# Both banks of a row tile in one loop over k, the second matmul of each pair asked to use the weights already in the array

## Chip, cores, metric

One core of a Trainium2 chip. The metric is the device time of one execution in microseconds (us); medians over several executions are quoted.

## The reference

```python
m, k, n = 4096, 4096, 4096
a, b, bias = randn(m, k), randn(k, n), randn(n)      # float32
out = np.tanh(np.matmul(a, b) + bias)
```

## The kernel before

The operands are cast to fp16 by the DMAs that load them. `a` is transposed on VectorE (DVE) and is the stationary operand: 128 x 128 weights per k tile, 32 k tiles (`KT`). `b` is the moving operand: a chunk of 1024 columns lies in SBUF, as `J` = 2 pieces of `NB` = 512 columns, for one `ps` tile in PSUM each (a bank, below). After a special start for the first eight row tiles, 120 row tiles follow (`todo`). Each takes one bank after the other: 32 matmuls of 512 columns into the first bank, 32 into the second. The k-th matmuls of both banks use the same weights, and each loads them for itself.

```python
    def mm(ps, at, bt, t, j, start, stop):
        nc.tensor.matmul(
            ps, at[:, t, :], bt[t // TB][:, t % TB, ts(j, NB)], start=start, stop=stop
        )

    def finish(ps, addend, mi, c0, w=NB, o_sb=None, pieces=1):
        ...                                  # DVE: add the bias out of PSUM; ACT: tanh; SP: store
    # ... the start: warm-up matmuls, first column chunk ...
    for i, (c, mi) in enumerate(todo):
        # ... loads of b and a for later row tiles ...
        if i + 2 < len(todo):
            new_at(i + 2)                    # DVE: transpose of the row tile after the next
        at = at_q.pop(0)
        for j in range(J):
            halves = 2 if i == len(todo) - 1 and j == J - 1 else 1
            w = NB // halves
            for h in range(halves):
                ps = psum.tile([P, w], fp32, name="ps")
                c0 = j * NB + h * w
                for t in range(KT):
                    nc.tensor.matmul(
                        ps,
                        at[:, t, :],
                        b_cur[t // TB][:, t % TB, ds(c0, w)],
                        start=t == 0,
                        stop=t == KT - 1,
                    )
                finish(ps, bias_bc[:, ds(c0, w)], mi, c * NCW + c0, w, pieces=halves)
```

## Time and profile before

| | before |
|---|---|
| time | 1792.26 us, median of 3 runs (1791.81 to 1792.65) |
| matmuls, weight loads in the trace | 8248, 8248 |
| start of one matmul to start of the next, 300 to 1700 us | 215 or 216 ns, mean 215.83 ns |
| 512 columns alone, at 0.4167 ns a column (2.4 GHz; worked out of four widths below) | 213.33 ns |

The page of the profile of before. The line of engines gives busy us, share of the span and number of instructions (PE is TensorE's matmuls, PEld its weight loads). q8 is the queue that brings instructions (packets, MB). The long line is the chain of waits that ended last, by share of the span. Then groups: line, engine, operation, output<-input, shapes, count, then busy us and mean ns of one, then idle time before.

```profile
span 1789.8 us, 19352 instructions
...
PE 1779.1 (99%) x8248; PEld 807.4 (45%) x8248; DVE 745.0 (42%) x420; ACT 162.7 (9%) x260; POOL 358.0 (20%) x668
...
q8 instruction: 64, 1.05, 0.2%
...
PE ps L321 92%; PE ps L121 2%; DMA b<-in_b_dram 2%; DMA an<-in_a_dram 1%; POOL b L66 0%; DMA bias_bc<-in_bias_dram 0%; POOL an L75 0%; DVE atx L83 0%; ACT o_sb L135 0%; DVE o_sb L132 0%; ACTq L354 0%; DVEq L132 0%; POOLq L343 0%
...
L321 PE MATMUL ps<-b,at 128*128 128x512 f16 x7712 | 1657.8, 378 | 0.0
L321 PEld LDWEIGHTS <-at 128*128 128x128 f16 x7712 | 754.6, 98 | 903.3
L132 DVE TENSOR_TENSOR o_sb<-ps,bias_bc 128x512 f32<-128x512 f32 (+1 forms) x243 | 166.4, 686 | 977.8 <-PE ps L321 764.1
```

The chain is 92% the matmuls of L321, the row tiles, and TensorE never idles there (0.0 us before the 7712 matmuls). A matmul's record lasts 378 ns in the mean, while matmuls start 215.83 ns apart: the records overlap, so their length says nothing about the rate. The rate is in the starts. This is the timeline of before between 500 and 503 us (start, duration, engine, group, count):

```profile
499.77 3.40 PE L321 MATMUL ps<-b,at 128*128 128x512 f16 x15
499.99 2.90 PEld L321 LDWEIGHTS <-at 128*128 128x128 f16 x14
```

Fifteen matmuls span 3.40 us, the last one's record of 379 ns included: (3.40 - 0.379) / 14 = 0.2158 us from start to start. The fourteen weight loads keep the same step, one for each matmul, 98 ns each.

VectorE's part of the timeline of before shows the order of its work, one addition per bank, some 6.9 us apart:

```profile
493.99 0.69 DVE L132 TENSOR_TENSOR o_sb<-ps,bias_bc 128x512 f32<-128x512 f32 x1 [1.86 <-issue]
500.89 0.69 DVE L132 TENSOR_TENSOR o_sb<-ps,bias_bc 128x512 f32<-128x512 f32 x1 [6.21 <-PE ps L321]
501.50 4.43 DVE L83 STREAM_TRANSPOSE at<-an 128x4096 f16<-128x4096 f16 x1
```

### The profile page before, as it was taken

The page shows a single profiled execution, that of the slowest core. Times are in us where ns is not written, and L with a number is a line of the kernel's source. Part 1 is how long each engine was busy: PE and PEld are TensorE (multiplying, and loading weights), DVE is VectorE, ACT ScalarE, POOL GpSimd, SP SyncE. Part 2 cuts the span into 40 slices and gives each one's busy share as a digit, 9 for nine tenths or more (in the row PEclk, how much of TensorE's full clock was granted, in tenths as well). Part 3 has the DMA queues.
Part 4 walks back from the last instruction along what each step waited for, and adds up shares of the span by engine and source line. Part 5 has one row for each costly group of instructions (what it writes and reads, how often), then busy time and mean ns, then how long its engine had stood idle before and what let it go on. Part 6 is the DMA issues. An engine that isn't in the chain of part 4 may idle for free.

```text
span 1789.8 us, 19352 instructions
## 1 busy us (share of the span) xinstructions
PE 1779.1 (99%) x8248; PEld 807.4 (45%) x8248; DVE 745.0 (42%) x420; ACT 162.7 (9%) x260; POOL 358.0 (20%) x668
## 2 busy tenths in 40 slices
PE   8999999999999999999999999999999999999999
PEld 3444444444444444444444444444444444444444
DVE  5463344334433444334433443344334433444341
ACT  0110000000000000000000000000000000000001
POOL 6422222211222211111132222111111111111100
PEclk9999999999999999999999999999999999999999
DMA  9999887665777865655588777555665555655621
GB/s 182 214 189 189 155 159 147 125 132 114 159 147 144 170 140 108 121 119 124 106 168 156 158 142 142 121 112 107 127 120 112 112 113 109 125 112 111 120 70 41
DMA packets 138630, 238.26 MB, mean 133 GB/s; under 512 B 14769, under 2 KB 27569, under 8 KB 138545
## 3 DMA queue, kind: packets, MB, share of 16 engines
q0 software_dynamic: 101248, 169.91, 56.6%
q1 hardware_dynamic: 37296, 67.13, 10.3%
q8 instruction: 64, 1.05, 0.2%
q14 instruction: 22, 0.17, 0.0%
HBM read 337.64 MB, written 67.11 MB: 226 GB/s over the span
## 4 chain that ended last, share of the span: by engine, by line
PE 95%; DMA 4%; POOL 1%; issue 1%; DVE 0%; ACT 0%; ACTq 0%; DVEq 0%; POOLq 0%
PE ps L321 92%; PE ps L121 2%; DMA b<-in_b_dram 2%; DMA an<-in_a_dram 1%; POOL b L66 0%; DMA bias_bc<-in_bias_dram 0%; POOL an L75 0%; DVE atx L83 0%; ACT o_sb L135 0%; DVE o_sb L132 0%; ACTq L354 0%; DVEq L132 0%; POOLq L343 0%
## 5 line engine op out<-in xcount | busy, mean ns | idle before, releaser
L321 PE MATMUL ps<-b,at 128*128 128x512 f16 x7712 | 1657.8, 378 | 0.0
L321 PEld LDWEIGHTS <-at 128*128 128x128 f16 x7712 | 754.6, 98 | 903.3
L132 DVE TENSOR_TENSOR o_sb<-ps,bias_bc 128x512 f32<-128x512 f32 (+1 forms) x243 | 166.4, 686 | 977.8 <-PE ps L321 764.1
L83 DVE STREAM_TRANSPOSE at<-an 128x4096 f16<-128x4096 f16 (+1 forms) x136 | 551.0, 4056 | 26.7 <-DMA an<-in_a_dram 26.7
L75 POOL DMA_DIRECT2D an<-in_a_dram x524 | 282.8, 547 | 1296.6 <-DVE at L83 1224.4
L135 ACT ACTIVATE o_sb<-o_sb 128x512 f32<-128x512 f32 (+1 forms) x243 | 151.5, 624 | 1505.7 <-DVE o_sb L132 1505.7
L66 POOL DMA_DIRECT2D b<-in_b_dram x136 | 73.2, 542 | 55.2 <-PE ps L321 28.6
L121 PE MATMUL ps<-b,at 128*128 128x512 f16 x256 | 58.6, 391 | 3.9 <-DMA b<-in_b_dram 2.9
L121 PE MATMUL ps<-b,atx 128*128 128x512 f16 x256 | 55.7, 379 | 1.3 <-DVE atx L83 1.3
L121 PEld LDWEIGHTS <-at 128*128 128x128 f16 x256 | 25.3, 100 | 37.1 <-issue 5.7
L121 PEld LDWEIGHTS <-atx 128*128 128x128 f16 x256 | 24.8, 98 | 32.2 <-DVE atx L83 2.7
L132 DVE TENSOR_TENSOR spill<-ps,spill 128x512 f32<-128x512 f32 x16 | 10.7, 684 | 25.7 <-PE ps L121 25.4
L135 ACT ACTIVATE spill<-spill 128x512 f32<-128x512 f32 x16 | 10.0, 630 | 117.2 <-DVE spill L132 117.2
L83 DVE STREAM_TRANSPOSE atx<-an 128x1024 f16<-128x1024 f16 (+1 forms) x8 | 18.3, 2295 | 0.0
L155 DVE TENSOR_TENSOR spill<-ps,bias_bc 128x512 f32<-128x512 f32 x16 | 10.1, 670 | 10.0 <-PE ps L121 10.0
L196 PE MATMUL ps<-zeros 128*128 128x512 f16 x24 | 7.3, 476 | 1.2 <-DVE zeros L193 1.2
L196 PEld LDWEIGHTS <-zeros 128*128 128x128 f16 x24 | 2.8, 118 | 5.2 <-issue 2.5
L90 POOL DMA_DIRECT2D bias_bc<-in_bias_dram x4 | 2.3, 563 | 0.1
L135 ACT ACT_TABLE_LOAD x1 | 1.3, 1283 | 0.7 <-PEq L343 0.7
L193 DVE MEMSET zeros<- 128x256 uint32 x1 | 0.3, 272 | 0.9 <-PEq L343 0.9
L343 POOL MEMSET const-float32-0.0<- 128x1 f32 x1 | 0.1, 98 | 0.2 <-issue 0.2
L343 POOL MEMSET const-bfloat16-1.0<- 128x1 bf16 x1 | 0.1, 101 | 0.0
(2 smaller groups left out, 0.2 us busy)
## 6 DMA issues: line engine op xcount, KB each, us to landing
an<-in_a_dram POOLq DMA_DIRECT2D x492, 256.0 KB, 5.4
out_dram<-o_sb SPq DMA_DIRECT2D x239, 256.0 KB, 4.3
b<-in_b_dram POOLq DMA_DIRECT2D x120, 256.0 KB, 8.9
out_dram<-spill SPq DMA_DIRECT2D x16, 256.0 KB, 6.4
an<-in_a_dram POOLq DMA_DIRECT2D x16, 192.0 KB, 7.8
an<-in_a_dram POOLq DMA_DIRECT2D x16, 128.0 KB, 5.7
b<-in_b_dram POOLq DMA_DIRECT2D x16, 128.0 KB, 5.0
bias_bc<-in_bias_dram POOLq DMA_DIRECT2D x4, 512.0 KB, 8.2
```

The costliest lines, as they stand in the source:

```text
L66: nc.gpsimd.dma_start(out=bt[t0 // TB][ds(q * QP, QP), ds(t0 % TB, nt), :], in_=src.rearrange("(t p) n -> p t n", p=QP),)
L75: nc.gpsimd.dma_start(out=an[ds(q * QP, QP), :, :], in_=src.rearrange("(mb p) k -> p mb k", p=QP),)
L83: nc.vector.transpose(at[:, ds(t0, nt), :].rearrange("P t (mb p) -> P mb t p", p=QP), an[:, ds(mb0, Q), :].rearrange("P mb (t k) -> P mb t ...
L90: nc.gpsimd.dma_start(out=bias_bc, in_=bass.AP(tensor=src.tensor, offset=src.offset, ap=[[0, P], *src.ap]),)
L121: nc.tensor.matmul(ps, at[:, t, :], bt[t // TB][:, t % TB, ts(j, NB)], start=start, stop=stop)
L132: nc.vector.tensor_tensor(out=o_sb[:, piece], in0=ps[:, piece], in1=addend[:, piece], op=mybir.AluOpType.add)
L135: nc.scalar.activation(o_sb[:, piece], o_sb[:, piece], mybir.ActivationFunctionType.Tanh)
L155: nc.vector.tensor_tensor(out=aside(m, j), in0=ps, in1=bias_bc[:, ts(j, NB)], op=mybir.AluOpType.add)
L193: nc.vector.memset(zeros, 0.0)
L196: nc.tensor.matmul(warm, zeros[:, :P], zeros, start=i == 0, stop=i == WARM - 1)
L321: nc.tensor.matmul(ps, at[:, t, :], b_cur[t // TB][:, t % TB, ds(c0, w)], start=t == 0, stop=t == KT - 1,)
L343: nc = _bacc.Bacc("TRN2", target_bir_lowering=False, num_devices=1)
```

## The change

Take both banks of a row tile through k together, so that the two matmuls with the same weights follow each other, and spare the second its weight load. The second is put in by hand as an instruction with `ldweights=False`. The last row tile stays as it was.

```diff
+    def mm_held(ps, at, bt, t, j, start, stop):
+
+        rhs = bt[t // TB][:, t % TB, ts(j, NB)]
+        nc.tensor.add_instruction(
+            mybir.InstMatmult(
+                name=nc.get_next_instruction_name(),
+                start_tensor_calc=start,
+                stop_tensor_calc=stop,
+                tile_size=(P, P),
+                tile_position=(0, 0),
+                ldweights=False,
+                ins=[
+                    nc.tensor.lower_ap(rhs, opt=False),
+                    nc.tensor.lower_ap(at[:, t, :], opt=False, for_matmul_weights=True),
+                ],
+                outs=[nc.tensor.lower_ap(ps)],
+            )
+        )
...
+        if i < len(todo) - 1:
+
+            pair = [psum.tile([P, NB], fp32, name="ps") for j in range(J)]
+            for t in range(KT):
+                mm(pair[0], at, b_cur, t, 0, t == 0, t == KT - 1)
+                mm_held(pair[1], at, b_cur, t, 1, t == 0, t == KT - 1)
+            for j in range(J):
+                finish(pair[j], bias_bc[:, ts(j, NB)], mi, c * NCW + j * NB)
+            continue
```

## The prediction

> What bounds the kernel now. The page of the profile gives TensorE 99% busy, and the chain of waits is 92% steady-state matmuls of the row tiles. Busy time says little for pipelined matmuls, so I read the spacing of their starts in the trace: between 300 and 1700 us they are 215 or 216 ns apart, mean 215.83 ns, with no longer gap even where one bank gives way to the next. The first column, where eight banks alternate, shows the same. The windows view shows a granted clock of 1.00, so 512 columns at 2.4 GHz[...] take 213.33 ns: the array streams 98.8% of the time, and 2.5 ns per matmul is left. The 256-column matmuls of the last piece are 109.2 ns apart, again 2.5 ns over their columns: a fixed cost per matmul. From 127.8 to 1782.1 us there is nothing but matmuls back to back; the rest is the start and some 8 us of tail, which the change leaves alone.

> What the change removes. 119 of 120 row tiles are paired: 119 x 32 = 3808 weight loads go. One takes 98 ns by the line's view, 373 us of 807 us in sum. But each starts 1.6 ns after a matmul starts and ends over 115 ns before the next: all hidden, so removing it gains nothing by itself. The only thing to win is the part of the 2.5 ns that belongs to changing weights, at most 3808 x 2.5 = 9.5 us (0.53%). [...] at the halved clock the first matmuls, which load weights too, are 426 or 427 ns apart, 512 columns at 1.2 GHz with nothing added; an array-side switch of six cycles would add 5 ns. So I expect a matmul without a load to cost the same 215.8 ns. No matmul of before goes without a load, which leaves it open.

> What the change moves. Both banks of a row tile end 0.2 us apart, not 6.9. VectorE then adds twice in a row (0.69 us each), ScalarE does two tanh (0.62), two stores go out together. VectorE is 42% busy and its order is unchanged, so the next transpose starts some 0.5 us later, with two row tiles (27.6 us) of slack. PSUM is four row tiles deep; no wait. The weights have at least 215 ns for a load of 98 ns. Tiles of b are released at most half a row tile earlier or later, double buffered. The last row tile is as before.

> On the critical path: only the spacing of the matmuls. Predicted 1791.5 us, range 1782 to 1794. Chances: faster by over 2% 0.01, within 2% 0.97, slower 0.02.

> What would show each step: some 4440 weight loads, busy near 434 us; matmul count as before; spacing of starts after a loaded and after a held matmul both 215.8 ns (if 213.3 for the held ones, then some 1783 us); no idle TensorE at row-tile ends; VectorE additions in pairs.

> What would make it wrong: a held matmul that cannot follow its neighbour as closely (each 10 ns would cost 38 us), a weight load that is not pulled ahead past a held matmul and is exposed, or extra semaphore waits from instructions put in by hand.

(1791.5 us is the time of before, measured at 1792.26 us, with nothing taken off for the loads, and the 1782 us of the range are those 1791.5 us less the 9.5 us. The 2.4 GHz were not read from a trace then, but the trace of before gives them: 215.83 ns at 512 columns less 109.17 ns at 256 (mean of the last 60 steps) are 106.67 ns for 256 columns, 0.4167 ns a column.)

## The result

After: 1791.10 us median of 4 runs (1790.47 to 1791.91). Before, on the same occasion: 1792.03 us (1791.03 to 1792.65, 4 runs). Ratio 0.9996, 95% interval 0.9978 to 1.0013: the same. A ratio here is the mean time of one kernel's fast runs over that of the other's fast runs of the same rounds, so it is not quite the ratio of the medians.

The page of the profile of after, the same parts as above (L121 is the ordinary matmul of a pair and some of the start, L128 the one put in by hand):

```profile
span 1788.7 us, 19352 instructions
...
PE 1777.7 (99%) x8248; PEld 807.2 (45%) x8248; DVE 733.8 (41%) x420; ACT 159.0 (9%) x260; POOL 358.0 (20%) x668
...
q8 instruction: 64, 1.05, 0.2%
...
PE ps L121 52%; PE ps L128 46%; PE ps L349 1%; DMA an<-in_a_dram 1%; DVE atx L83 0%; DVE at L83 0%; DVE spill L174 0%; POOL an L75 0%; ACT o_sb L154 0%; DVE o_sb L151 0%; ACTq L382 0%; DVEq L83 0%; DVEq L151 0%; DVE spill L151 0%; POOLq L371 0%
...
L121 PE MATMUL ps<-b,at 128*128 128x512 f16 x4064 | 1500.6, 379 | 4.2 <-DMA b<-in_b_dram 2.9
L128 PE MATMUL ps<-b,at 128*128 128x512 f16 x3808 | 1443.2, 379 | 0.0
L121 PEld LDWEIGHTS <-at 128*128 128x128 f16 x4064 | 397.6, 98 | 485.7 <-issue 4.7
L128 PEld LDWEIGHTS <-at 128*128 128x128 f16 x3808 | 372.6, 98 | 449.3
...
L151 DVE TENSOR_TENSOR o_sb<-ps,bias_bc 128x512 f32<-128x512 f32 (+1 forms) x243 | 155.0, 680 | 989.0 <-issue 969.5
```

This is the first thing to read, before any time: there are still 8248 weight loads, and 3808 of them carry the line of the matmul that was to have none. The instruction count (19352) and the instruction bytes (1.05 MB) have not moved either. The loop order did change. TensorE's weight loads in the timeline of after take both lines in turn:

```profile
499.93 0.10 PEld L128 LDWEIGHTS <-at 128*128 128x128 f16 x1
500.15 0.10 PEld L121 LDWEIGHTS <-at 128*128 128x128 f16 x1
500.36 0.10 PEld L128 LDWEIGHTS <-at 128*128 128x128 f16 x1
500.58 0.10 PEld L121 LDWEIGHTS <-at 128*128 128x128 f16 x1
```

And VectorE adds twice in a row at the end of each row tile (timeline of after), then transposes:

```profile
485.73 1.29 DVE L151 TENSOR_TENSOR o_sb<-ps,bias_bc 128x512 f32<-128x512 f32 x2 [8.17 <-issue]
486.93 4.43 DVE L83 STREAM_TRANSPOSE at<-an 128x4096 f16<-128x4096 f16 x1
499.54 1.29 DVE L151 TENSOR_TENSOR o_sb<-ps,bias_bc 128x512 f32<-128x512 f32 x2 [8.17 <-issue]
```

The pair takes 1.29 us where two single ones took 0.69 each; that is VectorE's 11 us less busy time (745.0 to 733.8), off the critical path. TensorE has 0.0 us of idle time before L128, and start to start is 215 or 216 ns, mean 215.83 ns, as before.

So the measured "same" answers another question than the one asked: it shows that the loop order costs nothing, and says nothing yet about a matmul without a load.

### The profile page after: what moved, and what is told of

Its sections match the earlier page's. It is cut to its first block, busy times and chain, and to the rows that moved or that the text cites. A ratio compares the mean times of both kernels' runs of the same rounds, so it can differ in the third digit from the quotient of the medians.

```text
span 1788.7 us, 19352 instructions
## 1 busy us (share of the span) xinstructions
PE 1777.7 (99%) x8248; PEld 807.2 (45%) x8248; DVE 733.8 (41%) x420; ACT 159.0 (9%) x260; POOL 358.0 (20%) x668
## 3 DMA queue, kind: packets, MB, share of 16 engines
q8 instruction: 64, 1.05, 0.2%
## 4 chain that ended last, share of the span: by engine, by line
PE 98%; DMA 1%; DVE 1%; issue 0%; POOL 0%; ACT 0%; ACTq 0%; DVEq 0%; POOLq 0%
PE ps L121 52%; PE ps L128 46%; PE ps L349 1%; DMA an<-in_a_dram 1%; DVE atx L83 0%; DVE at L83 0%; DVE spill L174 0%; POOL an L75 0%; ACT o_sb L154 0%; DVE o_sb L151 0%; ACTq L382 0%; DVEq L83 0%; DVEq L151 0%; DVE spill L151 0%; POOLq L371 0%
## 5 line engine op out<-in xcount | busy, mean ns | idle before, releaser
L121 PE MATMUL ps<-b,at 128*128 128x512 f16 x4064 | 1500.6, 379 | 4.2 <-DMA b<-in_b_dram 2.9
L128 PE MATMUL ps<-b,at 128*128 128x512 f16 x3808 | 1443.2, 379 | 0.0
L121 PEld LDWEIGHTS <-at 128*128 128x128 f16 x4064 | 397.6, 98 | 485.7 <-issue 4.7
L128 PEld LDWEIGHTS <-at 128*128 128x128 f16 x3808 | 372.6, 98 | 449.3
L151 DVE TENSOR_TENSOR o_sb<-ps,bias_bc 128x512 f32<-128x512 f32 (+1 forms) x243 | 155.0, 680 | 989.0 <-issue 969.5
L154 ACT ACTIVATE o_sb<-o_sb 128x512 f32<-128x512 f32 (+1 forms) x243 | 147.7, 625 | 1509.5 <-DVE o_sb L151 1509.5
L121 PE MATMUL ps<-b,atx 128*128 128x512 f16 x256 | 55.7, 379 | 1.3 <-DVE atx L83 1.3
L121 PEld LDWEIGHTS <-atx 128*128 128x128 f16 x256 | 24.8, 98 | 32.2 <-DVE atx L83 2.7
L349 PE MATMUL ps<-b,at 128*128 128x256 f16 (+1 forms) x96 | 14.1, 308 | 0.0
```

Source lines behind the costliest of these rows:

```text
L121: nc.tensor.matmul(ps, at[:, t, :], bt[t // TB][:, t % TB, ts(j, NB)], start=start, stop=stop)
L128: nc.tensor.add_instruction(mybir.InstMatmult(name=nc.get_next_instruction_name(), start_tensor_calc=start, stop_tensor_calc=stop, tile_si ...
L151: nc.vector.tensor_tensor(out=o_sb[:, piece], in0=ps[:, piece], in1=addend[:, piece], op=mybir.AluOpType.add)
L154: nc.scalar.activation(o_sb[:, piece], o_sb[:, piece], mybir.ActivationFunctionType.Tanh)
L349: nc.tensor.matmul(ps, at[:, t, :], b_cur[t // TB][:, t % TB, ds(c0, w)], start=t == 0, stop=t == KT - 1,)
```

## Experiments

Theory 1: the flag is not honoured when the program is built, so the changed kernel is only a change of loop order. Theory 2: even with the loads really gone nothing is won, because the 2.5 ns over the 512 columns belong to each matmul and not to changing weights. The rivals: the 2.5 ns are the price of changing weights (up to 9.5 us to win); or a load cannot be placed two matmuls ahead and the change would lose time.

All start-to-start figures below are differences of successive matmul starts in the trace between 300 and 1700 us:

```
kernel            columns   loads     mean ns   the commonest steps (count)
before              512      8248      215.83   216 (5402), 215 (1083)
after               512      8248      215.83   216 (5402), 215 (1084)
e0_plain_pairs      512      8248      215.83   216 (5402), 215 (1083)
e1_held             512      4440      215.83   216 (5402), 215 (1083)
e2_one_load         512       751      215.83   216 (5402), 215 (1084)
e3_two_loads        512     15864 *    215.83   216 (5403), 215 (1083)
e4_three_loads      512     23480 *    215.83   216 (5402), 215 (1083)
e5_narrow_loads     128     31096       55.83   56 (20892), 55 (4182)
e6_narrow_held      128      4440       55.83   56 (20893), 55 (4181)
e7_64_loads          64     61560       35.16   29 (31479), 30 (6261), 53 (925)
e8_64_held           64      4440       29.17   29 (40001), 30 (7998)
* in the built program; the trace records 8248
```

### e0: the loop order alone

```diff
-                mm_held(pair[1], at, b_cur, t, 1, t == 0, t == KT - 1)
+                mm(pair[1], at, b_cur, t, 1, t == 0, t == KT - 1)
```

> The changed loop order, but the second matmul of a pair is an ordinary one. Theory (the flag that asks for no load is not honoured when the program is built, so every matmul of the changed kernel still has a load): the built program is the same instruction for instruction as the changed kernel, 8248 weight loads, so 1791 us, within 1 us of the changed kernel. Rival (the flag does something on the chip that the count of loads does not show): a difference from 1791.1 us, or another spacing than 215.8 ns.

A listing of the two built programs was compared first: apart from line numbers, TensorE's instructions are the same in the same order, 8248 loads and 8248 matmuls, and so are those of the other engines. Measured: 1791.47 us (5 runs), ratio to before 1.0 (0.9987 to 1.0012). Theory 1 holds. The changed kernel with `ldweights=True`, and with the flag left away, builds to the same program once more: each time 8248 loads and the flag False on all 8248 matmuls. In these builds the flag changed nothing, whether given as False, as True or not at all.

### e1: the loads really taken out

The changed kernel, with the load before each `mm_held` deleted from the scheduled program (none of these loads held a wait or a signal, which the edit asserts):

```diff
+HELD = set()                       # names of the matmuls that mm_held puts in
+def edit_loads(nc):                # between the schedule and the launch
+    ...                            # for each block: out = [], load = None
+            for i in b.instructions:
+                if isinstance(i, mybir.InstLdweights):
+                    load = len(out)
+                elif isinstance(i, mybir.InstMatmult):
+                    if i.name in HELD:
+                        del out[load]
+                    load = None
+                out.append(i)
+            b.instructions = out
```

> The changed kernel with the 3808 loads really taken out of the scheduled program: 4440 loads, some 434 us of load time. If the 2.5 ns over the 512 columns is a fixed cost of every matmul (theory): spacing stays 215.8 ns, 1791 us, same as before within 0.1%. If it is the price of changing weights (rival 1): 213.3 ns before or after a held matmul, 1791 - 9.5 = 1782 us, 0.9947 of before. If the engine cannot place a load two matmuls ahead (rival 2): spacing over 216 ns at every second matmul, slower than 1795 us. The result must stay correct.

Measured: correct; 1792.36 us (1791.16 to 1794.66, 5 runs), ratio 1.0005 (0.9993 to 1.0018). Its page, the line of engines, and the instruction queue:

```profile
PE 1777.3 (99%) x8248; PEld 434.6 (24%) x4440; DVE 733.8 (41%) x420; ACT 159.0 (9%) x260; POOL 357.9 (20%) x668
...
q8 instruction: 49, 0.80, 0.2%
```

The loads are gone this time: 3808 fewer, load time nearly halved, and the result is still right, so a second matmul does find the weights in the array. Its timeline, matmuls:

```profile
500.03 0.38 PE L124 MATMUL ps<-b,at 128*128 128x512 f16 x1
500.25 0.38 PE L133 MATMUL ps<-b,at 128*128 128x512 f16 x1
500.47 0.38 PE L124 MATMUL ps<-b,at 128*128 128x512 f16 x1
500.68 0.38 PE L133 MATMUL ps<-b,at 128*128 128x512 f16 x1
```

and loads, one for each two matmuls:

```profile
500.25 0.10 PEld L124 LDWEIGHTS <-at 128*128 128x128 f16 x1 [0.33 <-issue]
500.68 0.10 PEld L124 LDWEIGHTS <-at 128*128 128x128 f16 x1 [0.33 <-issue]
```

L124 is the matmul that changes weights, L133 the one that keeps them. Both start 0.216 us after the one before them. Had a kept set of weights spared the 2.5 ns, two steps would take 429.2 ns; the loads are 431.67 ns apart in the mean. Theory 2 holds, and both rivals fall: the interval of the ratio excludes the 0.9947 of a price for changing weights, and no step is over 216 ns.

### e2: one load for 64 matmuls

```diff
-                mm(pair[0], at, b_cur, t, 0, t == 0, t == KT - 1)
+                (mm if t == 0 else mm_held)(pair[0], at, b_cur, t, 0, t == 0, t == KT - 1)
```

> Wrong result on purpose: one load for the 64 matmuls of a row tile, 751 loads in the whole program. Doubles the effect of e1. Fixed cost of every matmul: still 215.8 ns and 1791 us. Price of changing weights: 213.3 ns, 7497 x 2.5 = 18.7 us less, 1772 us (0.9895 of before).

Measured: wrong, as meant; 1792.21 us (5 runs), ratio 1.0004 (0.9990 to 1.0018), 215.83 ns. From its page:

```profile
PE 1778.3 (99%) x8248; PEld 73.9 (4%) x751; DVE 733.8 (41%) x420; ACT 159.0 (9%) x260; POOL 357.9 (20%) x668
```

Load time went from 45% of the span to 4% and the time stayed. It bounds what any reuse of weights could win in this kernel: at most 0.1% by the interval, and nothing by the spacing of the matmuls.

### e3 and e4: more loads than needed

The loads are kept, and one (e3) or two (e4) further loads of the same weights are put in front of each of the 7616 matmuls of pairs.

```diff
+                    if i.name in HELD:              # here: both matmuls of a pair
+                        for _ in range(EXTRA):      # 1 in e3, 2 in e4
+                            out.append(mybir.InstLdweights(name=..., engine=load.engine,
+                                ins=list(load.ins), outs=[], tile_size=(P, P), tile_position=(0, 0)))
```

> Each of the 7616 paired matmuls has its weights loaded twice, 15864 loads. If loads are hidden as long as they fit under a matmul (2 x 98 = 196 ns under 215.8): no change, 1791 us. If there is room for only one set of weights beside the ones in use, or a load that no matmul uses stops the next one: the second load waits for the next matmul and at least 98 ns are exposed per matmul, 7616 x 98 = 746 us more, some 2540 us.

> Three loads before each of the 7616 paired matmuls. With two loads (e3) the time did not move and the trace records one load a matmul, though the built program holds both. If each load in the program takes 98 ns of its own one after the other, three take 294 ns, 78 ns more than a matmul, and the time goes to about 1791 + 7616 x 0.078 = 2387 us. If a load that another load follows costs (nearly) nothing, 1791 us and again one record a matmul.

Measured: e3 1791.32 us, ratio 0.9999 (0.9985 to 1.0012); e4 1791.38 us, ratio 0.9994 (0.9977 to 1.0011); 4 runs each, both correct. The trace shows 8248 loads in both. The pages of e3 and of e4:

```profile
PE 1777.6 (99%) x8248; PEld 807.1 (45%) x8248; DVE 733.8 (41%) x420; ACT 159.0 (9%) x260; POOL 358.0 (20%) x668
...
q8 instruction: 94, 1.54, 0.3%
```

```profile
PE 1778.2 (99%) x8248; PEld 807.2 (45%) x8248; DVE 733.8 (41%) x420; ACT 159.1 (9%) x260; POOL 358.7 (20%) x668
...
q8 instruction: 124, 2.03, 0.5%
```

### e5 and e6: matmuls narrower than a load

Each matmul of a pair is cut into four of 128 columns into the same bank; in e5 each has its own load, in e6 all eight of a k share one.

```diff
-                mm(pair[0], at, b_cur, t, 0, t == 0, t == KT - 1)
-                mm_held(pair[1], at, b_cur, t, 1, t == 0, t == KT - 1)
+                for j in range(J):
+                    for n in range(0, NB, NW):      # NW = 128
+                        mm_held(pair[j], at, b_cur, t, j, n, t == 0, t == KT - 1, j + n > 0)
```

(The last argument says whether the load is taken out; it is left away in e5. Only the first piece of a bank is marked as its start.)

> Each 512-column matmul of a pair cut into four of 128 columns into the same bank, each with its own load (31096 loads): 53.3 ns of columns over a load of 98 ns that no longer fits under one matmul. Theory (loads cost nothing because they are shorter than the matmul above them): now they are exposed, spacing 98 ns or a little less, 30464 x 0.098 = 2985 us + 147 us = 3130 us[...]. If loads never cost anything: 55.8 ns, as e6.

> As e5, but one load for the eight 128-column matmuls of a k (4440 loads). With 2.5 ns as a fixed cost of each matmul: 53.33 + 2.5 = 55.83 ns, 30464 x 0.05583 = 1701 us in place of 7616 x 0.21583 = 1644 us: 1791 + 57 = 1848 us. If the 2.5 ns belonged to 512 columns (a pause in proportion to the columns streamed): no change, 1791 us. Against e5 this is what holding weights is worth where loads do not fit: expected well over 25%. The result must be correct in both.

Measured, 4 runs each, both correct: e5 1849.95 us, ratio 1.0323 (1.0307 to 1.0338); e6 1849.27 us, ratio 1.0317 (1.0301 to 1.0332). The time of e6 came as expected, 1848 us. The theory that e5 was to test fell, and so did the guess that e6 would beat it by well over 25%: they differ by 0.04%. From the page of e5, then of e6, the line of engines and the groups of the pairs:

```profile
PE 1835.9 (99%) x31096; PEld 1763.3 (95%) x31096; DVE 733.8 (40%) x420; ACT 159.0 (9%) x260; POOL 358.7 (19%) x668
...
L136 PE MATMUL ps<-b,at 128*128 128x128 f16 x30464 | 1701.1, 219 | 0.0
L136 PEld LDWEIGHTS <-at 128*128 128x128 f16 x30464 | 1701.0, 98 | 0.2
```

```profile
PE 1836.5 (99%) x31096; PEld 435.0 (24%) x4440; DVE 733.8 (40%) x420; ACT 159.0 (9%) x260; POOL 358.8 (19%) x668
...
L136 PE MATMUL ps<-b,at 128*128 128x128 f16 x30464 | 1701.1, 219 | 0.0
...
L136 PEld LDWEIGHTS <-at 128*128 128x128 f16 x3808 | 372.7, 98 | 1328.1 <-issue 1327.7
```

In e5 the loads are "busy" for the whole 1701 us, 95% of the span for the engine as a whole, yet they cost nothing: 30464 of 98 ns each would be 2985 us one after the other, so their records overlap. 98 ns is the length of one load's record, not how soon the next can start: they start 55.83 ns apart in the mean, as the matmuls do. By its record the load is not even over when its matmul starts: in the trace of e5 (300 to 1700 us) each load starts some 54 ns before its own matmul and its record ends 42 to 44 ns after the matmul's start, where in before it ends 116 to 118 ns ahead of it. (Seven of the eight loads of a k bring weights that are already there, but the eighth brings new ones, and no step is over 56 ns.) The matmuls' step is (128 + 6) / 2.4 = 55.83 ns in both kernels. The same sum, 6 cycles of 2.4 GHz over the columns, gives 215.83 ns at 512 columns, so the cost is per matmul and neither in proportion to the columns nor tied to weights.

### e7 and e8: 64 columns

```diff
-    NW = 128
+    NW = 64
```

(Against e5 for e7, and against e6 for e8.)

> As e5 with 64 columns a matmul, each with its own load (61560 loads). At 128 columns the loads, 98 ns each in the trace, started 55.8 ns apart and cost nothing, so a load's start-to-start time is at most 55.8 ns. At 64 columns a matmul alone would be 26.67 + 2.5 = 29.17 ns. If a load can also follow a load every 29 ns or less: 60928 x 0.02917 = 1777 us plus 147 us = 1925 us, same as e8. If a load's own start-to-start time lies between 29 and 55.8 ns, it is now the limit: between 1925 and 3547 us, and the spacing in the trace is that time.

> As e7, but one load for the sixteen 64-column matmuls of a k (4440 loads). If the 2.5 ns holds for each matmul: 29.17 ns and 1925 us. [...] The difference from e7 is the first size at which loads taken out could be worth something.

Measured, 4 runs each, both correct: e7 2290.04 us (2283.24 to 2302.32), ratio 1.2792 (1.2748 to 1.2836); e8 1926.35 us, ratio 1.0755 (1.0737 to 1.0773). e8 came as expected, (64 + 6) / 2.4 = 29.17 ns. The widths also give the clock by themselves: 55.83 - 29.17 = 26.67 ns for 64 columns more, and 215.83 - 55.83 = 160 ns for 384 more, are both 0.4167 ns a column, 2.4 GHz, with 2.5 ns left over a matmul. e7 is where taking out loads pays for the first time: 364 us between the medians. But the loads' own rate is not the reason. The commonest step in e7 is 29 ns, as in e8. The rest is in pauses; e7's timeline, matmuls:

```profile
494.81 1.56 PE L136 MATMUL ps<-b,at 128*128 128x64 f16 x48
498.42 7.91 PE L136 MATMUL ps<-b,at 128*128 128x64 f16 x256 [2.04 <-issue]
506.74 3.89 PE L136 MATMUL ps<-b,at 128*128 128x64 f16 x128 [0.40 <-issue]
512.67 17.51 PE L136 MATMUL ps<-b,at 128*128 128x64 f16 x542 [2.04 <-issue]
```

In brackets stands the idle time in front, up to 2 us, with no semaphore behind it. The two groups that lie whole between pauses hold 256 and 128 matmuls (the first and last are cut by the window), and for 226 of the 236 pairs of successive pauses in the trace the distance is a multiple of 128 matmuls: with a load for each, 256 instructions, 16 KB at the 64 bytes that e1, e3 and e4 show for a load. The instruction queue moves packets of that size (e7's page, then e8's):

```profile
q8 instruction: 481, 7.88, 1.4%
```

```profile
q8 instruction: 258, 4.23, 0.9%
```

7.88 MB in 481 packets is 16.4 KB each. Over the whole stretch of 64-column matmuls (127 to 2266 us) 237 pauses of over 200 ns cost 310 us over the normal step, and 2056 steps of 45 to 60 ns another 49 us; 64 columns at half the measured 2.4 GHz would take 64 / 1.2 = 53.3 ns, and the windows view of e7 grants 0.50 to a run of these steps (589.0 to 591.5 us). An estimate for all of them: 2056 x 53.3 ns = 110 us, and the run's mean clock of 0.975 over 2284.6 us is what 114 us at 0.50 and the rest at 1.00 would give. Sum: 60928 x 29.17 ns = 1777, plus 310, plus 49, plus some 147 us outside the paired row tiles (1791 less 7616 x 0.21583), 2283 us against the trace's span of 2284.6.

That the pauses are waits for instructions is the author's reading; the trace's records of the instruction queue fit it: every one of the 237 pauses ends 1.1 to 1.7 us after a packet of that queue has landed, whether the packet took 0.9 us or 2.1; only 11% of the ordinary steps fall into that interval after a landing. And in e5 and e8, where an instruction is due every 27 or 28 ns and not every 14.6 ns, no step is over 56 and 30 ns (300 to 1700 us). No run brings the instructions as fast as e7 without its loads, so this cause is supported by the traces and not shown by an edit of its own; why 1.1 us or more pass after the landing stays open.

## Why the prediction was right, and where it was not

- **The time.** Predicted 1791.5 us, within 2%; measured 1791.1 us. Right.
- **"3808 weight loads go", "some 4440 weight loads, busy near 434 us".** This step failed. None went: 8248 loads, 807.2 us. I took the flag in the diff at its word, and nothing in a reading of before could have shown otherwise. The sign that I had named for it, the count of loads, is what exposed it at once. e1 is the kernel that I had predicted: 4440 loads, 434.6 us.
- **"A matmul without a load costs the same 215.8 ns."** The run of after could not test it. e1 and e2 did: 215.83 ns with 4440 and with 751 loads, ratios 1.0005 and 1.0004. Right, and the at most 9.5 us that I left for the opposite case are 0.
- **"All hidden", because a load of 98 ns ends 115 ns before the next matmul.** The conclusion was right, the reason too narrow. e5 has a load of 98 ns for every 55.8 ns and hides it as well: by their records, loads overlap each other and last 42 to 44 ns past the start of the matmul that they serve. In this kernel the margin is greater than the 115 ns suggest: it still held in e5, with 98 ns of load to 55.8 ns of matmul.
- **The 2.5 ns as a fixed cost of each matmul.** Right, now at four widths: 6 cycles of 2.4 GHz over 512 (215.83 ns), 256 (109.17 ns, the mean of steps of 109 and 110 in the last piece of before), 128 (55.83 ns) and 64 columns (29.17 ns); at all but 256 with and without loads. The prediction's sign at the halved clock, steps of 426 or 427 ns with nothing added, is in the trace of before where the windows view grants 0.50 (12.1 to 13.7 us). In the first 5 us all steps but the first (402 ns) are the same but the view reads 1.00, so that the clock was halved there too is not shown by the view.
- **What moves.** Additions in pairs, no idle time of TensorE at row-tile ends, transposes in time: right, shown by the profile of after and by e0, which has this change alone.
- **What would make it wrong.** None of it happened; not even the really held matmuls of e1 follow less closely, and e1's loads start with the matmul right ahead of the one that needs them (500.25 us, the next L124 at 500.47 us).

The right time was therefore reached with one false step that happened to cost nothing: the loads that stayed are worth as much as the loads that would have gone. That it cost nothing was luck as far as the test goes: the time of after would have been the same had the step about matmuls without loads been wrong, and only e1 and e2 decide that step.

No version here beats the kernel before. What is left in its row tiles is 2.5 ns of 215.8 ns per matmul, which none of the edits here moves.

## What to carry to other kernels

Before explaining a time, count in the profile that the change took place: the number of records of what was to be removed, and the instruction bytes. For back-to-back matmuls read the step from start to start against the columns at the granted clock: if the step does not change when a load is taken out (55.83 ns in e5 and in e6), the load's busy time, even 95% of the span (e5), was worth nothing. Reuse of weights began to pay here only at 64 columns a matmul (e8 1926.35 us, e7 2290.04 us), and then, as far as the traces show, by nearly halving the instruction bytes (7.88 MB in e7, 4.23 MB in e8).
